# Hybrid encoder layer: output-projection weights, keys and values loaded into the low half of their split tiles, half results and x in four buffers each, and two instead of three value tiles ahead of the state-space output

## The chip, the cores and the metric

The kernel runs on one core of one Trainium2 chip. The metric is the device time of one execution in microseconds (us); lower is better. Times given here are the median of three runs, and one further execution was recorded by the hardware profiler. The engines are PE (TensorE: matrix products, with its weight loads shown apart as PEld), DVE (VectorE), ACT (ScalarE), POOL (GpSimd) and SP (SyncE, which only issues transfers). Each engine works through its own instructions in order. Sixteen DMA engines move the data.

## The reference

One layer on x of shape (1, 1024, 1024) in float32, three residual sub-layers. Only the first two matter here.

```python
h = rms_norm(x, mix_pre_g); proj = h @ w_in            # u 512 | q 512 | k 512 | v 512 | 8 gates
y_ssm = s5_mixer(u, ...)                               # diagonal state space, gelu, gated (glu)
y_fox = forgetting_attention(q, k, v, f_logit)         # 8 heads of 64, causal
y_mix = concatenate([rms_norm(y_ssm, ssm_out_g), rms_norm(y_fox, fox_out_g)])
x = x + rms_norm(y_mix @ w_out, mix_post_g)            # output projection
# cross-attention: 4 heads of 256, 256 memory tokens
kv = rms_norm(mem, mem_g) @ xa_wkv                     # keys | values
x = x + rms_norm(attention(rms_norm(x, xa_pre_g) @ xa_wq, k, v) @ xa_wo, xa_post_g)
x = x + rms_norm(swiglu(rms_norm(x, ffn_pre_g)), ffn_post_g)
```

## The kernel before, in words

**Products.** A float32 operand is split into a high and a low half (`split`, L112): ACT writes `hi` as a rounded copy (L113), DVE writes `lo = src - hi` (L115, or L117 with a gain). A product is three matmuls, hi·hi, hi·lo and lo·hi (`mm3`, L122 to L124). So each weight that is loaded needs one ACT and one DVE instruction before PE can use it.

**Order.** The kernel is written as generators that are stepped against each other. A framework then schedules all instructions by its own model of the engines and by priorities, and writes a fixed order for each engine; a changed buffer count or loop can move instructions far from the edit. SP issues the loads in that fixed order, and a load whose buffer is still in use holds every load behind it on SP. POOL issues the stores. On ACT and DVE, too, an instruction that waits holds all that follow.

**Buffers.** Tiles are taken from rings: `slab` 16 buffers (8 KB in each partition), `raw` 2 (weights as they are loaded), `whl` 3 (split weights), `a` 2, `b` 2, `c` 3, `d` 1, `e` 1, `t2` 3 (half as large, shown as `t` in the trace), four PSUM banks `g`, later four more named `x`. A ring's next tile waits until the last reader of the oldest one is done.

**Stages that the change touches**, in order of time:

1. *Projection in* (`in_proj`, L869). It ends with the generator `v1`, the second half of the value columns (8 tiles of 24 matmuls with 256 columns, evicted by ACT at L316 into a `t2` tile and stored), interleaved with `ssm_out` (L635): the state-space output, in two halves of four groups of matmuls (L643, L644), each half followed by gelu (L645) and transposes. The table V1_AT says how many value tiles go ahead of each step of `ssm_out`.
2. *Forgetting attention* (`fox`, L705): scores, exponential (L739), transposes (L758, evicted at L763), products with the values (L772). Into it are paced the `fillers` (L975), at 1.02 of their steps for one of the attention: the rest of `v1`, the gate `glu`, the state-space half of the output projection (`out_ssm`, evicted at L836 and stored to `t1_d`), the memory's keys and values (`mem_tile`, 16 weights `in_wkv` through `raw` or `e`, stored to `kv_d`), and the first part of the keys' product with the query weights (`build_a`).
3. *Output projection* (L1023 to L1083). Four weights `w_out_f` are loaded into `raw` (L1026) and split into slabs `wo`. For each of eight blocks n of 128 rows: the x tile is loaded into `c` (L1060), the half result t of stage 2 from `t1_d` into `a` or `b` (L1063, two transfers of 256 KB, shown as `t_d`), two products with `wo` are added to t (DVE, L1070), squared (ACT, L1072), multiplied by a gain row (POOL, L1074; loaded from `in_post_g`), and the normalised row is added to x (DVE, L1078). `value_weights` (L1033) is interleaved: values are loaded into a `t2` tile (L1035), split into a `b` or `e` tile and multiplied with `in_wo` weights.
4. The cross-attention and the feed-forward layer follow; the change does not touch their code.

Of the kernel before, what the change touches and what calls it, by code (L numbers as in the profile page):

```python
# [9 lines left out]
F32 = mybir.dt.float32  # L10
F32R = mybir.dt.float32r
# [23 lines left out]
MAGIC = 12582912.0  # L35
RATE = 1.02
HP = 16 * (L - 1)
V1_AT = (3, 1, 1, 1, 1)
HID = ("11", "12", "22", "S1", "S2", "S3", "S4")
EVB = 13  # L40
OPB = 10
# [11 lines left out]
def layer(ctx: ExitStack, tc: tile.TileContext, a, out):  # L53
# [15 lines left out]
    def slab(shape, dt=F32R):  # L69
        return slabp.tile(shape, dt, name="slab", tag="slab")  # L70
# [4 lines left out]
    def raw(shape):  # L75
        return rawp.tile(shape, F32, name="raw", tag="raw")
# [44 lines left out]
    def mm3(ps, lh, ll, rh, rl, first, last):  # L121
        pe.matmul(ps, lh, rh, start=first, stop=False)  # L122
        pe.matmul(ps, lh, rl, start=False, stop=False)  # L123
        pe.matmul(ps, ll, rh, start=False, stop=last)  # L124
# [21 lines left out]
        return last, done  # L146

    boost = 5000
    stA, stB, stC = pool, pool, pool

    def tables(name):
# [2 lines left out]
    def load_w(src, shape, first=0, stage=None):  # L154
        w = tt(stage, [P, D]) if stage else raw([P, D])
        hl = whl([P, 2, D])
        if not first:
            sp.dma_start(out=w, in_=src)
        for cs in (slice(0, first), slice(first, D)):
            if cs.start < cs.stop:  # L160
                if first:
                    sp.dma_start(out=w[:, cs], in_=src[:, cs])
                with tc.high_priority(offset=boost):
                    split(hl[:, 0, cs], hl[:, 1, cs], w[:, cs])
        v = hl.rearrange("p t (a b) -> p t a b", b=shape)
        return v[:, 0], v[:, 1]
# [15 lines left out]
    nc_d = dram.tile([NH, S], F32, name="nc_d")  # L182
    t1_d = dram.tile([L, NC, D], F32, name="t1_d")
    kv_d = dram.tile([16, P, 256], F32, name="kv_d")
    x1_d = dram.tile([NT, P, D], F32, name="x1_d")
    x2_d = dram.tile([NT, P, D], F32, name="x2_d")
    t_d = dram.tile([8, P, 4, 512], F32, name="t_d")
# [681 lines left out]
    def in_proj():  # L869
        r_mem.append(mem_stats())  # L870
        yield from k4
        for i in range(1, 4):
            yield from qk_tile(i + 4, xH, xL, rb)
        for n, _ in enumerate(v_tiles(0, xH, xL, r_x)):
            if n % 2:
                yield
        f_gate(gate[0])
        for i in range(4):
            yield from qk_tile(i, xH, xL, rb)
        drain(gs)  # L880
        go = ssm_out()
        for n in V1_AT:
            step(v1, n)
            step(go)
        drain(go)
# [107 lines left out]
    def build_a(c):  # L993
        for t in range(2):
            Ah[c, t], Al[c, t] = slab([P, 4, 512]), slab([P, 4, 512])
        for h in range(2):
            hd = 2 * c + h
            kr = t2t([P, 2, 256])
            sp.dma_start(out=kr, in_=kv_d[2 * hd:2 * hd + 2].rearrange("d p m -> p d m"))
            kh = tt(("ea", "ba")[c][h], [P, 2, 2, 256], F32R)  # L1000
            split(kh[:, 0], kh[:, 1], kr)
            wq = [load_w(a["wqT"][2 * hd + d], P) for d in range(2)]
            ms = slice(h * 256, h * 256 + 256)
            for ft in range(0, KT, 2):
# [17 lines left out]

    wo = []  # L1023
    for i in range(4):
        w = raw([P, D])
        sp.dma_start(out=w, in_=a["w_out_f"][i])  # L1026
        hl = slab([P, 2, D])
        split(hl[:, 0], hl[:, 1], w)
        wo.append(hl)
    g_mp = gain_row(0, "d")  # L1030
    VW = {}

    def value_weights(h):  # L1033
        vr = t2t([P, 2, 256])
        sp.dma_start(out=vr, in_=kv_d[8 + 2 * h:8 + 2 * h + 2].rearrange("d p m -> p d m"))  # L1035
        vh = tt("bebe"[h], [P, 2, 2, 256], F32R)
        split(vh[:, 0], vh[:, 1], vr)
        wo_ = [load_w(a["wo"][2 * h + d], 512) for d in range(2)]
        for mt in range(2):
            VW[2 * h + mt] = slab([P, 2, D])  # L1040
        for c in range(2):
            tiles = [(mt, (x_ps if h == 3 else g_ps)([P, 512])) for mt in range(2)]
            for d in range(2):
                for mt, ps in tiles:
                    ms = slice(mt * P, mt * P + P)
                    mm3(ps, vh[:, 0, d, ms], vh[:, 1, d, ms], wo_[d][0][:, c], wo_[d][1][:, c], d == 0, d == 1)
                    yield
            for mt, ps in tiles:
                split(VW[2 * h + mt][:, 0, c * 512:c * 512 + 512], VW[2 * h + mt][:, 1, c * 512:c * 512 + 512], ps)
# [6 lines left out]
    kept = {}  # L1056
    for n, j in enumerate((3, 4, 5, 6, 7, 0, 1, 2)):
        ts = slice(j * P, (j + 1) * P)
        xt = tt("c")
        sp.dma_start(out=xt, in_=a["x"][ts, :])  # L1060
        t = tt("aab"[n % 3])
        for i in range(2):
            sp.dma_start(out=t[64 * i:64 * i + 64], in_=t1_d.rearrange("j (k s) d -> s k j d", s=16)[2 * j + i])  # L1063
        ss4, ss, r = sm(4, "ss4"), sm(1, "ss"), sm(1, "r")
        for h in range(2):
            hs = slice(h * 512, h * 512 + 512)
            ps = x_ps([P, 512])
            for k in range(4):
                mm3(ps, yf[k][:, 0, ts], yf[k][:, 1, ts], wo[k][:, 0, hs], wo[k][:, 1, hs], k == 0, k == 3)
            dve.scalar_tensor_tensor(out=t[:, hs], in0=ps, scalar=r_f[:, j:j + 1], in1=t[:, hs], op0=ALU.mult, op1=ALU.add)  # L1070
# [558 lines left out]
```

## Time and profile before

| | |
|---|---|
| median of 3 runs | 1413.33 us |
| lowest, highest run | 1409.28, 1413.37 us |
| the profiled execution: time, span | 1414.33, 1412.5 us |
| mean granted TensorE clock in it | 0.992 |
| busy in the span: PE, DVE, ACT, POOL | 1381.8, 951.9, 652.3, 379.7 us |
| DMA moved | 239.45 MB, mean 170 GB/s |

The span runs from the first to the last instruction of the profiled execution; the time also holds what lies around it. Busy time is a sum over the span, so a full PE says nothing on a single stage: there, the timeline shows each instruction with the idle time ahead of it and the instruction that ended it. The granted clock is the share of TensorE's full speed that the chip's throttle allowed. The first state-space output matmul (L643) starts at 190.3 us and the last at 224.3, the attention's scores (L730) run from 235.2 on, its last product with the values (L772) is at 489.8, and the output projection's sums (L1070, into `a`) run from 501.6 to 550.1.

### The profile page before, as it was taken

How to read it: one execution, taken by the hardware profiler on the slowest of the kernel's cores; microseconds unless marked ns; L12 is line 12 of the kernel's file. 1: busy time of each engine (PE TensorE's matmuls, PEld its weight loads, DVE VectorE, ACT ScalarE, POOL GpSimd, SP SyncE). 2: the span in 40 equal slices, each digit the busy share in tenths (PEclk: the TensorE clock that was granted, in tenths of full speed). 3: DMA queues.
4: the chain of work that ended last, by engine and by line, in shares of the span. 5: the costliest groups of instructions: out<-in, count | busy, mean ns of one | idle time of the engine just before them, and what ended most of it. 6: DMA issues, size and time to landing. Idle time of an engine off the chain costs nothing.

```text
span 1412.5 us, 20273 instructions
## 1 busy us (share of the span) xinstructions
PE 1381.8 (98%) x7353; PEld 1163.3 (82%) x7353; DVE 951.9 (67%) x1719; ACT 652.3 (46%) x1289; POOL 379.7 (27%) x430
## 2 busy tenths in 40 slices
PE   9999989999999899999999999999999999999997
PEld 7889889789889677888888788888888888888886
DVE  8949944857567668545467777877776676655566
ACT  7383345766566546433344533333333334544351
POOL 0011110011211043001021367676766661000021
PEclk9999999999999999999999999999999999999999
DMA  6235665267663665024467345554444447955544
GB/s 217 91 108 163 201 220 138 69 200 213 183 180 113 175 194 186 27 75 152 161 202 257 97 176 193 178 187 161 145 158 154 165 150 236 357 196 194 179 164 164
DMA packets 104501, 239.45 MB, mean 170 GB/s; under 512 B 11464, under 2 KB 40136, under 8 KB 104272
## 3 DMA queue, kind: packets, MB, share of 16 engines
q1 hardware_dynamic: 85872, 176.24, 40.0%
q0 software_dynamic: 18528, 61.91, 12.3%
q8 instruction: 58, 0.95, 0.3%
q14 instruction: 43, 0.35, 0.1%
HBM read 169.43 MB, written 77.33 MB: 175 GB/s over the span
## 4 chain that ended last, share of the span: by engine, by line
PE 84%; DVE 7%; issue 3%; DMA 3%; ACT 2%; POOL 0%; SPq 0%; DVEq 0%; ACTq 0%; POOLq 0%
PE x L1294 17%; PE g L1294 13%; PE x L1557 7%; PE g L1557 7%; PE g L122 7%; PE g L124 7%; PE g L123 7%; PE x L123 2%; PE x L124 2%; PE g L758 2%; PE x L122 2%; PE g L772 2%; PE s L730 1%; PE s L731 1%; DMA a<-t_d 1%
## 5 line engine op out<-in xcount | busy, mean ns | idle before, releaser
L1294 PE MATMUL x<-slab,op 128*128 128x512 f32 x984 | 233.2, 389 | 0.5 <-DVE op L115 0.5
L1294 PEld LDWEIGHTS x<-slab,op 128*128 128x128 f32 x984 | 184.7, 188 | 39.2 <-DVE op L115 1.0
L1294 PE MATMUL g<-slab,op 128*128 128x512 f32 x744 | 178.7, 389 | 0.0
L115 DVE TENSOR_TENSOR slab<-slab 128x1024 fp32r<-128x1024 f32 (+2 forms) x92 | 110.2, 1207 | 86.4 <-ACT slab L113 85.2
L1294 PEld LDWEIGHTS g<-slab,op 128*128 128x128 f32 x744 | 139.7, 188 | 29.0
L122 PE MATMUL g<-slab,whl 128*128 128x512 f32 (+1 forms) x416 | 151.4, 364 | 0.8 <-ACT slab L485 0.4
L124 PE MATMUL g<-slab,whl 128*128 128x512 f32 (+1 forms) x416 | 148.7, 358 | 0.0
L123 PE MATMUL g<-slab,whl 128*128 128x512 f32 (+1 forms) x416 | 148.3, 357 | 0.0
L113 ACT ACTIVATE slab<-slab 128x1024 fp32r<-128x1024 f32 (+2 forms) x92 | 94.7, 1036 | 108.6 <-DMA slab<-hs_d 80.8
L1557 PE MATMUL g<-slab 128*128 128x512 f32 x462 | 126.6, 389 | 0.0
L1557 PE MATMUL x<-slab 128*128 128x512 f32 x462 | 126.6, 389 | 0.0
L1557 PEld LDWEIGHTS g<-slab 128*128 128x128 f32 x462 | 86.7, 188 | 18.0
L1557 PEld LDWEIGHTS x<-slab 128*128 128x128 f32 x462 | 86.7, 188 | 18.0
L115 DVE TENSOR_TENSOR op<-slab,op 128x512 fp32r<-128x512 f32 x80 | 84.6, 1068 | 11.5 <-ACT op L113 11.3
L1370 POOL TENSOR_TENSOR wt<-wt 128x256 f32<-128x256 f32 x88 | 83.1, 944 | 21.0 <-DMA wt<-in_w_down 17.4
L122 PE MATMUL g<-whl,slab 128*128 128x256 f32 (+2 forms) x288 | 86.8, 310 | 1.7 <-ACT yt L318 0.7
L122 PEld LDWEIGHTS g<-slab,whl 128*128 128x128 f32 x416 | 78.6, 189 | 12.0 <-ACT whl L113 0.6
L124 PEld LDWEIGHTS g<-slab,whl 128*128 128x128 f32 x416 | 78.4, 189 | 11.6 <-DVE whl L115 0.2
L123 PEld LDWEIGHTS g<-slab,whl 128*128 128x128 f32 x416 | 78.6, 189 | 10.6
L113 ACT ACTIVATE op<-slab 128x512 fp32r<-128x512 f32 x80 | 50.0, 628 | 79.9 <-PE g L1294 38.0
L124 PE MATMUL g<-whl,slab 128*128 128x256 f32 (+2 forms) x288 | 86.0, 299 | 0.0
L123 PE MATMUL g<-whl,slab 128*128 128x256 f32 (+2 forms) x288 | 85.7, 298 | 0.0
(397 smaller groups left out, 2890.3 us busy)
## 6 DMA issues: line engine op xcount, KB each, us to landing
hs_d<-ev POOLq DMA_DIRECT2D x77, 256.0 KB, 2.6
slab<-hs_d SPq DMA_DIRECT2D x35, 512.0 KB
wt<-in_w_down SPq DMA_DIRECT2D x44, 256.0 KB
wt_d<-wt POOLq DMA_DIRECT2D x22, 512.0 KB, 5.1
slab<-in_w_gate SPq DMA_DIRECT2D x20, 512.0 KB
slab<-in_w_up SPq DMA_DIRECT2D x20, 512.0 KB
slab<-wt_d SPq DMA_DIRECT2D x20, 512.0 KB
wd_d<-in_w_down SPq DMA_DIRECT2D x33, 256.0 KB
```

The lines of the kernel that those rows point to most:

```text
L113: first = act.activation(out=hi, in_=src, func=AF.Copy, scale=1.0 if mul is None else mul)
L115: (lo_eng or dve).tensor_tensor(out=lo, in0=src, in1=hi.bitcast(F32), op=ALU.subtract)
L122: pe.matmul(ps, lh, rh, start=first, stop=False)
L123: pe.matmul(ps, lh, rl, start=False, stop=False)
L124: pe.matmul(ps, ll, rh, start=False, stop=last)
L730: pe.matmul(ps[:, c0:c1], qt, ka[:, 0, c0:c1], start=True, stop=False)
L731: pe.matmul(ps[:, c0:c1], qt, ka[:, 1, c0:c1], start=False, stop=not dg)
L758: pe.transpose(tp[:, k], sc[:, (k0 + k) * P:(k0 + k + 1) * P], ident)
L772: pe.matmul(yp[hh * 64:hh * 64 + 64, c0:], w, pts[2 * hp + hh, qc][:, k, c0:], start=k == 0, stop=k == nk - 1, tile_position=(0, 64 * hh))
L1294: pe.matmul(ps, x[:, k], y[:, k], start=first and k + n == 0, stop=k == 3 and n == 2, skip_group_check=not first)
L1370: pool.tensor_tensor(out=o, in0=x, in1=y, op=ALU.subtract)
L1557: pe.matmul(banks[n][j], xo[:, u, js], wo[:, v], start=ends[0] and k == 0, stop=ends[1] and k == 2, skip_group_check=onto is not None)
```

## The change

Four edits.

- V1_AT is (2, 1, 1, 1, 1) in place of (3, 1, 1, 1, 1): two value tiles go ahead of the first state-space output; the last value tile is done as a filler of the attention.
- A DRAM tensor `wof_d` gets a copy of the four `w_out_f` weights, DRAM to DRAM, issued on SP after the last load of a `w_f` weight in the front. In stage 3 the weights are loaded from it into the low half of their slab and split in place, without `raw`.
- Keys are loaded into the low half of their split tile (an `e`, `a` or `b` tile), values into a `t2` tile that becomes their low half, with a second `t2` tile for the high half. Before, both went through a `t2` tile of their own, and the values' halves lay in a `b` or `e` tile.
- In the output projection the half results alternate over the rings `a` and `b` (2 + 2 buffers; before `a`, `a`, `b`), and x uses `e` for every fourth block and `c` for the others (1 + 3; before `c` alone). These loads are ordered behind the last load of the output weights.

```diff
-V1_AT = (3, 1, 1, 1, 1)
+V1_AT = (2, 1, 1, 1, 1)
...
+    fetched = []
...
         if not first:
-            sp.dma_start(out=w, in_=src)
+            fetched.append(sp.dma_start(out=w, in_=src))
...
+    wof_d = dram.tile([4, P, D], F32, name="wof_d")
...
         for i in range(1, 4):
             yield from qk_tile(i + 4, xH, xL, rb)
+            if i == 3:
+                with tc.issue_after(fetched[-1].ins):
+                    for j in range(4):
+                        sp.dma_start(out=wof_d[j], in_=a["w_out_f"][j])
...
-            kr = t2t([P, 2, 256])
+            kh = tt(("ea", "ba")[c][h], [P, 2, 2, 256], F32R)
+            kr = kh[:, 1].bitcast(F32)
             sp.dma_start(out=kr, in_=kv_d[2 * hd:2 * hd + 2].rearrange("d p m -> p d m"))
-            kh = tt(("ea", "ba")[c][h], [P, 2, 2, 256], F32R)
             split(kh[:, 0], kh[:, 1], kr)
...
     for i in range(4):
-        w = raw([P, D])
-        sp.dma_start(out=w, in_=a["w_out_f"][i])
         hl = slab([P, 2, D])
+        w = hl[:, 1].bitcast(F32)
+        wo_read = sp.dma_start(out=w, in_=wof_d[i])
         split(hl[:, 0], hl[:, 1], w)
...
-        vr = t2t([P, 2, 256])
+        vh, vl = t2t([P, 2, 256], F32R), t2t([P, 2, 256], F32R)
+        vr = vl.bitcast(F32)
         sp.dma_start(out=vr, in_=kv_d[8 + 2 * h:8 + 2 * h + 2].rearrange("d p m -> p d m"))
-        vh = tt("bebe"[h], [P, 2, 2, 256], F32R)
-        split(vh[:, 0], vh[:, 1], vr)
+        split(vh, vl, vr)
...
-        xt = tt("c")
-        sp.dma_start(out=xt, in_=a["x"][ts, :])
-        t = tt("aab"[n % 3])
-        for i in range(2):
-            sp.dma_start(out=t[64 * i:64 * i + 64], in_=t1_d...[2 * j + i])
+        t = tt("ab"[n % 2])
+        with tc.issue_after(wo_read.ins) if n else ExitStack():
+            for i in range(2):
+                sp.dma_start(out=t[64 * i:64 * i + 64], in_=t1_d...[2 * j + i])
+        xt = tt("ec"[n % 4 > 0])
+        with tc.issue_after(wo_read.ins):
+            sp.dma_start(out=xt, in_=a["x"][ts, :])
```

In the changed kernel line numbers are higher: L316 is L318, L645 is L647, L739 is L741, L763 is L765, L836 is L838, L1026 is L1033, L1060 is L1071, L1063 is L1068, L1070 is L1078, L1078 is L1086.

How the order moves at the places that the prediction speaks of follows; a row is an instruction's place in its engine's order, its line, operation, tiles and shape.

ACT at the end of stage 1, before: three value tiles (L316; `t` is the `t2` ring) are evicted ahead of the first gelu (L645).

```order
106 L113 ACTIVATE t_1939<-a 128x512
107 L316 ACTIVATE t_1985<-g,r_x 128x256
108 L626 ACTIVATE slab<-b 64x8x112 x2
109 L316 ACTIVATE t_2013<-g,r_x 128x256
110 L316 ACTIVATE t_2041<-g,r_x 128x256
111 L645 ACT_TABLE_LOAD
112 L645 ACTIVATE slab<-g 128x4x8x16 x4
113 L316 ACTIVATE t_2110<-g,r_x 128x256
```

The same place after:

```order
106 L113 ACTIVATE t_1944<-a 128x512
107 L318 ACTIVATE t_1990<-g,r_x 128x256
108 L628 ACTIVATE slab<-b 64x8x112 x2
109 L318 ACTIVATE t_2018<-g,r_x 128x256
110 L647 ACT_TABLE_LOAD
111 L647 ACTIVATE slab<-g 128x4x8x16 x4
112 L318 ACTIVATE t_2087<-g,r_x 128x256
```

One eviction fewer stands ahead of the gelu. On PE the order before is 49 value matmuls, eight pairs of L643 and L644, 10 value matmuls, four pairs, 13 value matmuls, four pairs; after, it is 25, twelve pairs, 23, four pairs.

ACT in stage 2, at the first split of a `wkv` weight (`whl<-raw`), before:

```order
185 L782 ACTIVATE d<-g 128x256
186 L836 ACTIVATE t_2720<-g,r_s 128x256 x2
187 L836 ACTIVATE t_2837<-g,r_s 128x256
188 L763 ACTIVATE slab<-g 128x4x128
189 L113 ACTIVATE whl<-raw 128x1024
190 L739 ACTIVATE c,nlr<-c,nlr 128x896
```

After:

```order
183 L784 ACTIVATE d<-g 128x256
184 L137 ACTIVATE rsy<-sv_s,epsc 128x8
185 L138 ACTIVATE rsy<-rsy 128x8
186 L765 ACTIVATE slab<-g 128x4x128
187 L113 ACTIVATE whl<-raw 128x1024
188 L741 ACTIVATE c,nlr<-c,nlr 128x896
189 L838 ACTIVATE t_2739<-g,r_s 128x256 x2
```

The L836 (now L838) evictions moved from ahead of the split to behind it.

SP between stages 2 and 3, before:

```order
101 L1063 DMA a<-t_d 64x1x1024 x2
102 L1026 DMA raw<-in_w_out_f 128x1024
103 L1035 DMA t_6060<-kv_d 128x2x256
104 L1063 DMA b<-t_d 64x1x1024 x2
105 L1060 DMA c<-in_x 128x1024 x2
106 L1063 DMA a<-t_d 64x1x1024 x2
107 L1026 DMA raw<-in_w_out_f 128x1024 x2
108 L158 DMA raw<-in_wo 128x1024
109 L1060 DMA c<-in_x 128x1024
110 L158 DMA raw<-in_wo 128x1024 x4
111 L947 DMA d<-in_post_g 128x1024
```

After:

```order
99 L1068 DMA a<-t_d 64x1x1024 x2
100 L159 DMA raw<-in_wo 128x1024 x2
101 L1033 DMA slab<-wof_d 128x1024 x4
102 L1071 DMA e<-in_x 128x1024
103 L1068 DMA b<-t_d 64x1x1024 x2
104 L1071 DMA c<-in_x 128x1024 x2
105 L1068 DMA b<-t_d 64x1x1024 x2
106 L1071 DMA c<-in_x 128x1024
107 L1068 DMA a<-t_d 64x1x1024 x2
108 L159 DMA raw<-in_wo 128x1024 x2
109 L953 DMA d<-in_post_g 128x1024
```

The four output weights stand together ahead of all x loads and of all but the first half result; four blocks of x and half results are now ahead of the later `in_wo` weights and of the gain row.

More of the change, by code (lines that the diff above doesn't have):

```diff
@@ L1045, in value_weights @@
                     ms = slice(mt * P, mt * P + P)
-                    mm3(ps, vh[:, 0, d, ms], vh[:, 1, d, ms], wo_[d][0][:, c], wo_[d][1][:, c], d == 0, d == 1)
+                    mm3(ps, vh[:, d, ms], vl[:, d, ms], wo_[d][0][:, c], wo_[d][1][:, c], d == 0, d == 1)
                     yield
@@ L1058, in layer @@
         ts = slice(j * P, (j + 1) * P)
-        xt = tt("c")
-        sp.dma_start(out=xt, in_=a["x"][ts, :])
-        t = tt("aab"[n % 3])
-        for i in range(2):
-            sp.dma_start(out=t[64 * i:64 * i + 64], in_=t1_d.rearrange("j (k s) d -> s k j d", s=16)[2 * j + i])
+        t = tt("ab"[n % 2])
+        with tc.issue_after(wo_read.ins) if n else ExitStack():
+            for i in range(2):
+                sp.dma_start(out=t[64 * i:64 * i + 64], in_=t1_d.rearrange("j (k s) d -> s k j d", s=16)[2 * j + i])
+        xt = tt("ec"[n % 4 > 0])
+        with tc.issue_after(wo_read.ins):
+            sp.dma_start(out=xt, in_=a["x"][ts, :])
         ss4, ss, r = sm(4, "ss4"), sm(1, "ss"), sm(1, "r")
```

## Prediction

> **What bounds the kernel now.** I read the engine table first.
>
> ```profile
> span 1412.5 us, 20273 instructions
> PE 1381.8 (98%) x7353; PEld 1163.3 (82%) x7353; DVE 951.9 (67%) x1719; ACT 652.3 (46%) x1289; POOL 379.7 (27%) x430
> ```
>
> TensorE is busy 98% of the span. The change adds or removes no arithmetic, so it can only touch what PE loses: idle time (at most 1412.5 − 1381.8 = 30.7 us) and time at a reduced clock. So I next listed the waits by engine, with PE first, and then the tensor engine's timeline for the row behind each of those gaps. The bracket is the idle time ahead of the row and who ended it.
>
> ```profile
> 184.47 0.28 PE L122 MATMUL g<-whl,slab 128*128 128x256 f32 x1
> 184.59 0.28 PE L123 MATMUL g<-whl,slab 128*128 128x256 f32 x1
> ...
> 190.35 0.39 PE L643 MATMUL g<-slab 128*128 128x128 f32 x2
> ...
> 190.79 0.39 PE L643 MATMUL g<-slab 128*128 128x128 f32 x2
> ...
> 198.60 0.80 PE L643 MATMUL g<-slab 128*128 128x128 f32 x2 [3.33 <-ACT t L316]
> 205.36 0.49 PE L643 MATMUL g<-slab 128*128 128x128 f32 x2 [0.56 <-ACT t L316]
> 207.88 0.39 PE L122 MATMUL g<-whl,slab 128*128 128x256 f32 x1 [0.46 <-ACT slab L645]
> ...
> 282.47 0.66 PE L758 MATMUL g<-ident,c 128*128 128x128 f32 x4 [1.51 <-ACT d L782]
> 289.51 1.11 PE L772 MATMUL g<-slab 128*64 128x256 f32 x4 [2.37 <-ACT t L836]
> ...
> 487.22 1.29 PE L772 MATMUL g<-slab 128*64 128x256 f32 x6 [1.54 <-ACT slab L763]
> 523.34 0.50 PE L122 MATMUL x<-slab 128*128 128x512 f32 x1 [1.87 <-DVE a L1070]
> 549.13 0.80 PE L122 MATMUL g<-whl,b 128*128 128x512 f32 x1 [2.00 <-DVE slab L115]
> ```
>
> A 256-column matmul starts every 0.12 us (184.47, 184.59), and a pair of L643 and L644 rows takes 0.44 us (190.35 to 190.79), so a v tile of 24 matmuls is 2.88 us and an output group of four pairs 1.78 us. Short gaps also cost clock. The table of stretches shows it (us; busy time and count of each engine; granted clock; DMA share, GB/s):
>
> ```profile
> 195.00:200.00 5.00, 1.67 (x9) 1.47 (x8) 0.00 (x0) 0.47 (x1) 0.54 (x1) 0.74 1.03 419
> 475.00:480.00 5.00, 5.00 (x38) 3.79 (x35) 3.97 (x7) 1.93 (x5) 0.00 (x0) 1.00 0.94 286
> 485.00:490.00 5.00, 3.46 (x21) 2.18 (x20) 2.89 (x2) 2.17 (x4) 1.49 (x1) 0.75 0.46 142
> 490.00:495.00 5.00, 5.00 (x23) 4.16 (x23) 2.17 (x3) 2.75 (x4) 0.24 (x1) 0.90 0.76 241
> 550.00:555.00 5.00, 4.21 (x14) 2.51 (x13) 5.00 (x9) 3.97 (x13) 1.28 (x1) 0.76 0.36 116
> ```
>
> **The change part by part. Two v tiles ahead.** The stall at 198.60 waits for L316, the eviction of a v tile. The chain of waits says what that eviction waited for:
>
> ```profile
> 189.63 8.34 DMA qk_d<-t
> ...
> 198.07 0.48 ACT t L316
> ...
> 202.38 0.21 PE g L124
> ...
> 207.23 0.61 ACT slab L645
> ```
>
> The eviction wants a `t` tile whose write to DRAM lands at 197.97. The third v tile and the last output groups stand behind it. After the change the order on PE is: one v tile and one matmul, three groups, the other 23 matmuls, the fourth group, and so on; the fourth group takes the bank that the second v tile leaves. I replay this. The first tile and one matmul end at 184.47 + 25 × 0.12 = 187.5. The first group needs its T matrix, which in the old run was there by 190.35 at the latest; I take the middle, 189.0. Three groups end at 194.3, the 23 matmuls at 197.1. The fourth group cannot start before the same write lands and the eviction is done: 198.07 + 0.48 = 198.55. It ends at 201.1 (between 200.3 at full clock and 202.3 at the pace of the old one, which took from 198.60 to 202.38). The gelu of its result then frees a bank 0.65 us later, as from 207.23 to 207.88. So v tile three starts at 201.8, where the old kernel starts tile four at 207.88. The deferred tile still has to be done: 2.88 us later. Gain 207.88 − 201.8 − 2.88 = **3.2 us**, with ends 2.0 and 4.0. Nothing is gained if a later buffer of the same ring is written late too.
>
> **Where the tile goes.** The fillers start with it, so everything after it moves by one tile against the attention. On ACT the first split of a `wkv` weight now stands ahead of an exponential and of L836 evictions that used to be before it. In the old run that split waits for its transfer:
>
> ```profile
> 281.32 4.87 DMA raw<-in_wkv
> 286.22 1.06 ACT whl L113
> ```
>
> ACT does nothing while it waits, and PE then waits for L836 (2.37 us at 289.51). With fewer evictions done before it, the same wait holds more of the four `g` banks. The two gaps here sum to 3.9 us; the reshuffle could heal 1.5 of it (the first gap) or add 3 (the excess of the 4.87 us transfer over the 1.51 us gap, rounded down). I take a loss of **1.0 us**.
>
> **Output weights by copy, into the slab.** In the old run the third and fourth loads wait for one of two `raw` buffers and stand on the SP queue behind loads of x and half results:
>
> ```profile
> 470.06 3.38 SPq L1060 DMA_DIRECT2D c<-in_x  x2
> 474.52 1.22 SPq L1063 DMA_DIRECT2D a<-t_d  x2
> 475.84 1.23 SPq L1026 DMA_DIRECT2D raw<-in_w_out_f  x2
> 484.41 1.06 ACT L113 ACTIVATE slab<-raw 128x1024 fp32r<-128x1024 f32 x1 [6.41 <-DMA raw<-in_w_out_f]
> 486.58 0.59 ACT L763 ACTIVATE slab<-g 128x512 f32<-128x512 f32 x1
> ```
>
> ACT stands 6.41 us at that split with L763 behind it, and PE's gap at 487.22 is L763's. Now the four loads need only their slab, stand together ahead of x, and L763 stands ahead of the last two splits on ACT. The gap goes: 5.00 − 3.46 = 1.54 us, and the clock behind it, 0.25 × 3.46 + 0.10 × 5.00 = 1.37 us. Together **2.9 us**; low end 1.5 if another wait throttles the clock there anyway. The order of the splits on DVE is the same four, so no work is added.
>
> The copy itself (four transfers of 512 KB, read and written) is issued once the last `w_f` weight of the front is fetched, and the queues there are empty:
>
> ```profile
> 55.00:60.00 5.00, 5.00 (x23) 4.13 (x22) 5.00 (x6) 0.75 (x2) 0.00 (x0) 1.00 0.03 7
> 60.00:65.00 5.00, 5.00 (x31) 4.42 (x30) 4.97 (x3) 1.74 (x5) 0.00 (x0) 1.00 0.00 0
> 67.19 8.88 SPq L328 DMA_DIRECT2D raw<-in_w_v  x2
> ```
>
> I cost it at nothing. Its cover is this empty stretch; 4.2 MB at the 419 GB/s of the busiest row above is 10 us, and that is what it could delay the next weights by if the stretch were not empty.
>
> **Half results and x in four buffers each.** The half result `t` had three buffers, and its last transfers came late, one of them here:
>
> ```profile
> 532.69 7.37 DMA a<-t_d
> DVE a L1070 <- DMA a<-t_d: 6.6, 2, 5.7
> 525.00:545.00 20.00, 20.00 (x89) 16.53 (x89) 15.84 (x27) 10.25 (x37) 10.54 (x10) 1.00 0.75 231
> 545.00:555.00 10.00, 7.14 (x23) 4.33 (x21) 9.75 (x17) 7.76 (x25) 4.49 (x3) 0.83 0.52 178
> ```
>
> The second row (waits between 500 and 560 us: total, times, longest) says that VectorE lost 6.6 us to these loads. It feeds both PE gaps: the one at 523.34 directly (L1070), and those from 549 on through its backlog, for it is idle for 4 us before 545 and full (9.75 of 10 us) after it. With two buffers more, loads four to eight are issued one block earlier. The prize is 1.87 us, 10.00 − 7.14 = 2.86 us of idle from 545 to 555 and 0.17 × 7.14 = 1.2 us of clock there, together 5.9 us. Against it: VectorE remains the fullest engine behind PE here and works in order, and the new order puts four loads of x and six of half results ahead of the later `wo` weights and of the gain row. If the weights come late instead, the loss is bounded by the nearest row, a gap like that of 549 (2 us). Between 5.9 gained and 2 lost I take two thirds of the prize, **4.0 us**, since the row of 6.6 us exceeds what is to be healed.
>
> **Keys and values in place.** No instruction is added: the load goes to the half that the split later overwrites. Values now hold two of three `t2` tiles until their matmuls end, so the next value load waits for the one before it; keys hold their `a`, `b` or `e` buffer from the load on. The cover is work PE has in hand, as the 20.00 us of 20.00 from 525 to 545 show. From 0 to 2 lost (a gap like 549's); I take **0.5 us**.
>
> **Sum.** −3.2 + 1.0 − 2.9 − 4.0 + 0.5 = −8.6 us on the profiled execution's 1414.33 us (1.8 us of it outside the span): 1405.7. That execution lies 1.0 us above the median of 1413.33, and one of the three runs at 1409.28, so I say **1406 us**. A change below 0.3% (4.2 us) cannot be told from none.
>
> **The clock, by the skill.** After a gap of 1.54 us the granted clock fell to 0.75, after 2.00 us to 0.76. The Trainium skill, "TensorE: Matmul & The Clock Gate", section "HAM oscillation — how this bites in real kernels", gives as its rule that only idle gaps longer than about 3.4 us throttle. None of the gaps above is that long, so this case's trace does not agree.
>
> **Rivals.**
> - *Gaps cost idle time alone* (the clock dips whatever the order). Then the front gives its change of idle: 3.33 + 0.56 + 0.46 before, 1.5 + 1.45 after, so −1.4; the rest is +1.0 − 1.5 − 3.2 (two thirds of 4.73) + 0.5. Sum −4.6: **1410**. For it: the low clock at 195 began inside a gap. Against it: each row with a reduced clock above holds or follows a gap. The rule named above would lead here. Chance 0.05.
> - *All of it lands*: −4.0 − 1.5 − 2.9 − 5.9 + 0 = −14.3, so **1400 to 1402**. For it: the gaps have one cause each. Against it: ACT's wait for `wkv` is still there and has more behind it. 0.15.
> - *VectorE, not the loads, holds the output projection.* It is 9.75 of 10 us busy at 545. Then only 1 us of the 5.9 is gained, and the front gives its low end: −2.0 + 1.0 − 2.9 − 1 + 0.5 = −4.4 and, with ACT's wait on `wkv` at its +3, −2.4: **1410 to 1412**. 0.27.
> - *Slower: the bunched loads starve the value weights.* Four loads of x (512 KB) and six of half results (256 KB) are 3.7 MB; at the 286 GB/s of the row at 475 they take 13 us, and the fourth `wo` weight and the gain row stand behind them. It decides once these come later than PE uses them now; the present loads are issued here:
>
> ```profile
> 488.42 11.44 SPq L158 DMA_DIRECT2D raw<-in_wo  x4
> 499.95 0.38 SPq L947 DMA_DIRECT2D d<-in_post_g  x1
> ```
>
>   Issued from 476 on, as the last pair of output weights was, the bunch ends at 489, and a weight of 4.87 us (the `wkv` row, the same size) is there by 494, ahead of the 499 at which the present four are issued. At the 142 GB/s of the row at 485 the bunch ends at 502 and the weight lands at 507: PE stands for 8 us, with 2.5 us of clock behind it (0.25 of ten). Then −3.2 + 1.0 − 2.9 + 10.5 = +5.4 us, **1420**. Against it: three of the weights are now fetched before the bunch. The Trainium skill, "DMA: Bandwidth & Descriptors", section "Issuing engines are not separate DMA queues", speaks for it: all transfers share the same 16 engines and interleave, so loads that start earlier take their bandwidth from others; the row at 475, 0.94 of the share, agrees that there is no slack there. 0.10.
>
> **Numbers.** The forecast, sum −8.6, has 0.43; its own range is 1403 to 1409. With the whole gain (0.15) and a fifth of the VectorE case, faster by over 0.3% (below 1409.1) is 0.63; within 0.3% 0.27; slower 0.10. The range from 1400 to 1414 leaves out the slower rival and about as much again at its two ends.
>
> **What would show it.** Right: in the changed profile the wait of ACT for the `raw` load is gone at 484 and no PE row of L772 waits for L763 there; the wait of VectorE for half results is below 2 us; the front's fourth group starts at 198 to 199 with a gap under 2 us ahead of it, and the fox attention's first rows come 3 us earlier relative to the work done. Wrong: a gap behind L836 or the first `wkv` split above 4 us, a PE row between 490 and 515 that waits for `whl` or a value load, or a VectorE that is still full behind 545.

## The result, and the profile after

| | before | after |
|---|---|---|
| median of the runs on one chip | 1410.48 us (8 runs) | 1417.12 us (8 runs) |
| lowest, highest | 1405.75, 1413.39 | 1415.19, 1422.13 |
| the profiled execution: time, span | 1414.33, 1412.5 | 1418.36, 1416.6 |

The ratio is 1.0051, 95% interval 1.0031 to 1.0072: the change is **slower by some 7 us**. The forecast was 1406 us, the range 1400 to 1414. The prediction expected four gaps on PE to shrink. Those at 198, 487 and 523 did; in place of the fourth, at 549, stood one of 11.07 us.

The engine table of the page of the changed kernel:

```profile
span 1416.6 us, 20283 instructions
PE 1378.9 (97%) x7353; PEld 1161.8 (82%) x7353; DVE 951.5 (67%) x1719; ACT 652.0 (46%) x1289; POOL 381.9 (27%) x430
```

PE has the same 7353 matmuls and is busy 37.7 us short of its span, where it was 30.7. The tensor engine's timeline of the changed kernel, the rows with a gap that answer to those shown of before:

```profile
190.43 0.46 PE L645 MATMUL g<-slab 128*128 128x128 f32 x2 [1.47 <-DMA slab<-T_d]
199.34 0.49 PE L645 MATMUL g<-slab 128*128 128x128 f32 x2 [0.56 <-ACT t L318]
201.86 0.38 PE L122 MATMUL g<-whl,slab 128*128 128x256 f32 x1 [0.46 <-ACT slab L647]
...
274.92 0.50 PE L732 MATMUL s<-slab,a 128*128 128x512 f32 x1 [1.99 <-DVE nlr L739]
...
285.94 0.40 PE L760 MATMUL g<-ident,c 128*128 128x128 f32 x1 [2.48 <-ACT t L838]
...
518.59 0.73 PE L124 MATMUL g<-whl,t 128*128 128x512 f32 x2 [0.79 <-DVE t L115]
550.58 0.79 PE L122 MATMUL g<-whl,t 128*128 128x512 f32 x1 [11.07 <-ACT t L113]
...
761.25 0.50 PE L122 MATMUL g<-slab,whl 128*128 128x512 f32 x1 [0.39 <-ACT whl L113]
```

The last row is the same instruction in both kernels; before it stood here:

```profile
756.93 0.50 PE L122 MATMUL g<-slab,whl 128*128 128x512 f32 x1 [0.39 <-ACT whl L113]
```

From 757 (761) on the two executions run alike: 1412.5 − 756.93 = 655.6 us to the end before, 1416.6 − 761.25 = 655.4 after. Of the 4.3 us between the rows, 1.3 have nothing to do with the change: they are there at 127 us (a short gap of PE ahead of the same matmul stands at 127.10 and 128.44), and 1.2 of them already where SP issues the `w_f` loads (42.00 and 43.24), ahead of the copy at 50.17. The other 3.0 us are the change in these two executions.

The new gap of 11.07 us is the largest of the whole program. PE waits there for the split of a value tile (`t<-t`, L113). The value had long been loaded; ACT came late to it. SP's, ACT's and DVE's timelines of the changed kernel:

```profile
528.14 0.38 SPq L1006 DMA_DIRECT2D a<-kv_d  x1
...
540.56 0.63 ACT L113 ACTIVATE a<-a 128x512 fp32r<-128x512 f32 x1 [10.19 <-DMA a<-kv_d]
549.91 0.61 ACT L113 ACTIVATE t<-t 128x512 fp32r<-128x512 f32 x1
...
541.23 0.69 DVE L115 TENSOR_TENSOR a<-a 128x512 fp32r<-128x512 f32 x1 [10.47 <-ACT a L113]
```

ACT stood for 10.19 us and DVE for 10.47 us at the split of the fourth key, `a<-a`, which waited for its load. The view of line L1006 gives the time from issue to landing (least, median, most) for two of the four key loads in this kernel, those into `a`:

```profile
DMA to landing us min/median/max: 2.6/7.5/12.3
```

The load of 528.14 is the one of 12.3 us: it lands at 540.4. The one of 2.6 us is the second key's, issued at 441.20. The load of 528.14 could not be issued earlier, for an `a` tile that holds a half result came free only then (its last reader, L1086, starts at 526.83 and takes 1.28 us). The stretches around it (us; busy time and count of PE, PEld, DVE, ACT, POOL; granted clock; DMA share, GB/s):

```profile
485.00:490.00 5.00, 5.00 (x34) 4.21 (x31) 1.58 (x4) 1.22 (x3) 0.74 (x1) 1.00 0.99 283
...
520.00:525.00 5.00, 5.00 (x24) 4.14 (x23) 3.68 (x10) 2.47 (x11) 3.69 (x4) 1.00 1.00 357
525.00:530.00 5.00, 5.00 (x24) 4.14 (x23) 4.47 (x8) 2.76 (x11) 3.06 (x3) 1.00 0.90 238
...
535.00:540.00 5.00, 4.51 (x20) 3.39 (x19) 0.00 (x0) 0.00 (x0) 0.00 (x0) 1.00 0.63 206
540.00:545.00 5.00, 0.00 (x0) 0.00 (x0) 3.65 (x7) 2.87 (x8) 1.35 (x1) 0.71 0.02 7
545.00:550.00 5.00, 0.00 (x0) 0.00 (x0) 3.81 (x9) 3.31 (x13) 1.99 (x2) 0.50 0.62 197
550.00:555.00 5.00, 4.42 (x10) 3.42 (x11) 4.88 (x7) 2.86 (x8) 4.26 (x2) 0.50 0.04 12
555.00:560.00 5.00, 5.00 (x27) 4.34 (x26) 3.39 (x6) 3.98 (x8) 0.20 (x1) 0.93 0.68 210
```

From 535 to 540 nothing runs but PE, on work it had in hand; then PE runs out. The DMA engines are full or nearly so when the key's load is issued (shares of 1.00 and 0.90); later in its flight they are not (0.74 and 0.63 in the two stretches from 530 to 540). The gap costs 11.1 us and the clock after it 0.50 × 4.42 + 0.07 × 5.00 = 2.6 us.

Why the split stood there is a matter of order. ACT's order of the changed kernel at the place (no time is in it):

```
425 L113 ACTIVATE slab<-g 128x512
426 L1080 ACTIVATE yt,ss_5712<-b 128x256 x2
427 L113 ACTIVATE a<-a 128x512
428 L137 ACTIVATE rsy<-ss,epsc 128x1
...
433 L113 ACTIVATE b<-b 128x512
...
437 L1080 ACTIVATE yt,ss_5842<-b 128x256 x2
438 L113 ACTIVATE t_5906<-t_5907 128x512
```

The split of the fourth key (427) is ahead of the squares of the last two blocks (L1080) and of the value's split (438), though nothing needs that key before the output projection is over. In the kernel before, keys came through a spare `t2` tile. The fourth key's load and its split there:

```profile
526.72 0.38 SPq L999 DMA_DIRECT2D t<-kv_d  x1
...
548.50 0.63 ACT L113 ACTIVATE a<-t 128x512 fp32r<-128x512 f32 x1 [0.95 <-DVE c L1078]
```

The load was issued only 1.4 us earlier than in the changed kernel; but its split stood 22 us behind it and waited for no load. So it is the place of the split, more than the time of the load, that changed. The first key is held in the changed kernel too: its split at 379.76 kept ACT waiting for 4.52 us, and PE was busy throughout (5.00 of 5.00 us in each stretch from 365 to 380).

### The profile page after: what moved, and what is told of

It is laid out like the page before. It is cut to its first block, busy times and chain, and to the rows that moved or that the text cites. A ratio compares the mean times of both kernels' runs of the same rounds, so it can differ in the third digit from the quotient of the medians.

```text
span 1416.6 us, 20283 instructions
## 1 busy us (share of the span) xinstructions
PE 1378.9 (97%) x7353; PEld 1161.8 (82%) x7353; DVE 951.5 (67%) x1719; ACT 652.0 (46%) x1289; POOL 381.9 (27%) x430
## 3 DMA queue, kind: packets, MB, share of 16 engines
q0 software_dynamic: 18528, 61.91, 12.3%
## 4 chain that ended last, share of the span: by engine, by line
PE 59%; DVE 0%; ACT 0%; issue 0%; DVEq 0%; ACTq 0%
PE x L1302 17%; PE g L1302 13%; PE x L1565 7%; PE g L1565 7%; PE g L124 2%; PE g L122 2%; PE g L123 2%; PE x L123 2%; PE x L124 2%; PE x L122 2%; PE g L1098 1%; PE g L1209 1%; DVE whl L115 0%; ACT whl L113 0%; DVE x L1545 0%
## 5 line engine op out<-in xcount | busy, mean ns | idle before, releaser
L115 DVE TENSOR_TENSOR slab<-slab 128x1024 fp32r<-128x1024 f32 (+2 forms) x96 | 115.3, 1208 | 85.9 <-ACT slab L113 83.9
L113 ACT ACTIVATE slab<-slab 128x1024 fp32r<-128x1024 f32 (+2 forms) x96 | 99.1, 1037 | 108.4 <-DMA slab<-hs_d 79.2
L113 ACT ACTIVATE op<-slab 128x512 fp32r<-128x512 f32 x80 | 50.0, 628 | 80.1 <-PE x L1302 38.2
```

What stands on the lines that cost most here:

```text
L113: first = act.activation(out=hi, in_=src, func=AF.Copy, scale=1.0 if mul is None else mul)
L115: (lo_eng or dve).tensor_tensor(out=lo, in0=src, in1=hi.bitcast(F32), op=ALU.subtract)
```

## The experiments

Two theories were set against each other first. **BLOCK**: the fourth key's split stands in ACT's and DVE's order ahead of work that is due, and holds it until the key's late load lands. **BUNCH** (the prediction's slower rival in a wider form): the loads brought forward fill the DMA engines, so whatever is needed next comes late.

### Key splits late

Loads, buffers and their order as in the changed kernel; the splits of keys three and four stand behind the output projection's last row on ACT and DVE.

```diff
+            with ExitStack() as late:
+                for ins in x1_row:              # last Exp and last x row of the loop over n
+                    late.enter_context(tc.issue_after(ins.ins))
                 split(kh[:, 0], kh[:, 1], kr)
```

> The changed kernel with one thing moved: the splits of the third and fourth keys stand on ACT and DVE behind the last row of the output projection; all loads, their order and buffers are as in the changed kernel. Theory BLOCK (the fourth key's load is issued only when its `a` buffer comes free at 528 us, lands 12 us later, and ACT and DVE, which work in order, stand at its split with the squares, the value split and the row sums behind it): the gap of 11.1 us at 550.6 falls below 3 us and its loss of clock (0.5 x 4.4 + 0.07 x 5 = 2.5 us) with it; 1417 - 10 to 13 = 1404 to 1407 us. Theory BUNCH (the earlier loads of x and half results fill the DMA engines, so what is needed next is late whatever stands in front of it): the loads are untouched, so a gap of 5 us or more stays between 530 and 560; 1411 to 1418 us.

Measured: **0.9972** of the kernel before (0.9958 to 0.9986), 1407.66 us beside 1411.53. Against the changed kernel that is 0.9972 / 1.0051 = 0.992, or 11 us. SP's row for the key, its time to landing, and PE's row at the old gap:

```profile
527.19 0.38 SPq L1006 DMA_DIRECT2D a<-kv_d  x1
...
DMA to landing us min/median/max: 2.7/7.6/12.5
...
540.29 0.50 PE L122 MATMUL g<-whl,t 128*128 128x512 f32 x1 [1.74 <-ACT t L113]
```

The load is as late as before the move (12.5 us) and the gap is 1.74 us instead of 11.07. The order of all instructions on SP, POOL and PE is the same in both kernels; on ACT the two splits are all that moved, on DVE three neighbours shifted by a few places with them. So BLOCK is shown, and BUNCH as the cause of this gap falls: the late load does no harm by itself. The time came out 0.7 us above the range that BLOCK gave.

### Keys back, keys and values back, four buffers back

```diff
-            kh = tt(("ea", "ba")[c][h], ...); kr = kh[:, 1].bitcast(F32)
+            kr = t2t([P, 2, 256]); ...; kh = tt(("ea", "ba")[c][h], ...)
```

> The changed kernel with the keys loaded into a `t2` tile again, as before the change; values, output weights, four buffers and two v tiles stay. BLOCK: the key load no longer waits for an `a` buffer, but `t2` has three buffers and each pair of value halves takes two, so keys and values now wait for each other; gap gone if the loads come early enough: 1404 to 1408 us. BUNCH: stall of 5 us or more stays: 1411 to 1418 us.

Measured: 0.9990 (0.9972 to 1.0008), 1410.0 us; 0.6% below the changed kernel. The time lies between the two ranges; no gap of 5 us is left, which speaks against BUNCH. The gaps left on PE in the output projection are short:

```profile
518.67 0.73 PE L124 MATMUL g<-whl,t 128*128 128x512 f32 x2 [1.42 <-DVE t L115]
541.47 0.50 PE L122 MATMUL g<-whl,t 128*128 128x512 f32 x1 [1.88 <-ACT t L113]
```

With the values' code undone as well (`vr` in a `t2` tile, halves in `b` or `e`):

> The changed kernel with keys and values as before the change (a `t2` tile each, split into `b` or `e`); output weights, four buffers and two v tiles stay. If the in-place keys are the whole of the loss: 1403 to 1407 us, faster than the kernel before by 0.3 to 0.5%. If the values in place were worth something of their own: slower than the run with only the keys back. BUNCH: 1411 to 1418 us.

Measured: 1.0020 (1.0004 to 1.0037), 1414.84 us: slower than with only the keys back, so the values' new place is worth something beside the four buffers, whose half results and x now go through `b` and `e` as well. The time is in BUNCH's range, but no gap of 5 us is there. The profiled execution was the slowest of its kernel, 1420.08 us:

```profile
524.24 0.79 PE L122 MATMUL x<-slab 128*128 128x512 f32 x1 [3.66 <-DVE b L1078]
...
553.00 0.50 PE L122 MATMUL g<-whl,b 128*128 128x512 f32 x1 [2.57 <-DVE slab L115]
```

And the loop over n with its old tiles (`c` for x, `a`, `a`, `b` for t), all else changed:

> The changed kernel with three buffers each for half results and x again (order of loads as before the change); keys and values in place stay. BUNCH: the stall near 550 goes, 1406 to 1410 us. BLOCK: the fourth key still has to wait for an `a` buffer behind the half results, and its load lands late: a gap of 4 us or more stays and the old gaps at 523 and 549 come back, 1412 to 1420 us.

Measured: 1.0007 (0.9991 to 1.0022), 1413.1 us. Both theories missed here: the time lies in BLOCK's range, but by luck, for none of the gaps that it named is there. The gap near 550 is 2.1 us (at 542.98), near what BUNCH had, but not because less was loaded: SP's order of this kernel has the fourth key's load behind all half results, and its split behind them on ACT. The time is not what BUNCH had, since another gap came up:

```profile
476.96 1.22 PE L122 MATMUL x<-slab 128*128 128x512 f32 x4 [2.50 <-ACT slab L113]
...
542.98 0.79 PE L122 MATMUL g<-whl,t 128*128 128x512 f32 x1 [2.11 <-ACT t L113]
```

So the block at 550 is made by two edits together: keys in place, and the order that came with the four buffers.

### Each part alone on the kernel before

The table alone:

```diff
-V1_AT = (3, 1, 1, 1, 1)
+V1_AT = (2, 1, 1, 1, 1)
```

> The kernel before with V1_AT = (2, 1, 1, 1, 1) alone. Theory FRONT (the traces of the changed kernel and of its variants): the deferred value tile saves 4.4 us by 208 us and the attention's first weeks of work, 265 to 295 us, give back 1.6 to 2.4 us by waits and a lower clock; net 2 to 3 us: 1408 to 1410 us beside 1411.5, 0.998 to 0.9985. Rival: the tile's time is only moved and the waits behind it take all of it: 1411 to 1412 us, ratio 1.

Measured: 1.0008 (0.9991 to 1.0024). The gain is not there. Its timeline and one stretch:

```profile
189.53 0.46 PE L643 MATMUL g<-slab 128*128 128x128 f32 x2 [1.91 <-DVE b L624]
202.58 0.39 PE L122 MATMUL g<-whl,slab 128*128 128x256 f32 x1 [0.46 <-ACT slab L645]
190.00:195.00 5.00, 5.00 (x32) 5.00 (x32) 1.79 (x3) 2.03 (x3) 1.68 (x4) 0.66 0.96 276
```

After a gap of 1.91 us the clock was 0.66; in the changed kernel 1.47 us came ahead of the same group, and the third value tile began 0.7 us earlier (201.86), although that execution ran 1.3 us late up to there.

The output weights alone (copy, load into the slab, split in place):

> The kernel before with the output weights by copy into the slab alone. Theory: ACT's wait of 6.4 us at 484 goes and with it PE's gap of 1.5 us and the clock behind it, 2.9 us: 1408 to 1409.5 us, and the copy at 50 to 60 us costs nothing. Rival: with x and half results in three buffers and not held behind the output weights, these loads still come late, in another place: 1411 to 1413 us.

Measured: 0.9990 (0.9971 to 1.0010), 1411.05 us: nothing that can be told from zero, and in the rival's range. It also showed something in the front, where its order is that of the kernel before:

```profile
196.15 0.49 PE L645 MATMUL g<-slab 128*128 128x128 f32 x2 [0.34 <-ACT t L318]
195.63 0.47 ACT L318 ACTIVATE t<-g,r_x 128x256 f32<-128x256 f32 x1 [2.93 <-DMA qk_d<-t]
```

The gap of 3.33 us, on which the first term of the prediction rests, is 0.34 us here. The write that ends it was issued at 190.17 and the eviction that waits for it started 5.5 us later; in the profile of before it was 8.4 us (189.63, 198.07).

Four buffers alone (the loop over n alone, with the rings `a`, `b` and `e`, `c`):

> The kernel before with half results alternating over `a` and `b` and x over `e` and `c` alone. Theory COLLIDE (the run with keys and values back was 1414.8 us although it has the gains of the front and of the output weights, 5 us): the split values are in `b` and `e`, which are now rings of half results and x as well, so loads wait for values and the reverse; slower than before, 1414 to 1420 us, with gaps of 3 us or more between 515 and 560. Theory of the prediction (two more buffers bring the loads forward): 1406 to 1408 us.

Measured: 1.0024 (1.0009 to 1.0040), slower. PE's largest gap in the loop is the value tile's, in `e`:

```profile
539.91 0.69 PE L122 MATMUL g<-whl,e 128*128 128x512 f32 x1 [4.28 <-ACT e L113]
```

Keys and values in place alone:

> The kernel before with keys and values loaded into the low half of their split tiles alone. If the in-place key blocks only where its load stands among the half results of the new order: the fourth key's load stands behind all of them here, no gap over 4 us between 520 and 560, 1408 to 1412 us. If it blocks by itself: a gap of 5 us or more there, 1414 to 1420 us.

Measured: **1.0053** (1.0033 to 1.0073), 1418.24 us: as slow as the whole change. The time is in the second range, but the gap at 523 stays under the 5 us named there, and no expectation named the gap in the attention. PE's gaps, and ACT's row in the attention:

```profile
370.92 0.39 PE L122 MATMUL g<-whl,slab 128*128 128x256 f32 x1 [3.07 <-ACT t L836]
...
523.86 0.79 PE L122 MATMUL x<-slab 128*128 128x512 f32 x1 [4.33 <-DVE a L1070]
...
369.39 0.63 ACT L113 ACTIVATE e<-e 128x512 fp32r<-128x512 f32 x1 [6.43 <-DMA e<-kv_d]
```

The first key, loaded in place into `e`, holds ACT for 6.4 us in the middle of the attention, with an eviction (L836) behind it that PE wants: the same block at another key. From 360 to 380 us idle time and reduced clock (reckoned as after the gap above, by stretches of five us) cost 4.5 us here and nothing in the kernel before. The gap at 523 is at the place of the old one of late half results, and longer: in the second profile of the kernel before, shown below, PE came to this place at 519.3, here at 519.5, and waited 2.48 us there and 4.33 here. From 500 to 570 idle time and clock cost 12.6 us, against 6.2 and 6.6 in the two profiles of before. The third key's split held ACT for 3.65 us in that stretch (at 529.94) without a gap on PE. This kernel's orders differ from before's in many places from 440 on, and how the 6 us more come about is not shown.

### The front's gap again, and the table beside the late splits

> The kernel before, unchanged, for a second profile. Open since the run with the output weights alone: its order in the front is that of the kernel before, but its gap ahead of the third group of L643 was 0.3 us instead of 3.3, since the write that the eviction waits for landed 3 us earlier. If that landing is the kernel's own: 3 to 4 us again at 198. If it varies between executions: another gap, 0 to 3 us, and the gain of the two v tiles, measured against one profile, is partly luck.

The kernel before, a second profile:

```profile
198.63 0.80 PE L643 MATMUL g<-slab 128*128 128x128 f32 x2 [2.86 <-ACT t L316]
...
521.75 0.50 PE L122 MATMUL x<-slab 128*128 128x512 f32 x1 [2.48 <-DVE a L1070]
```

The execution took 1412.52 us. The gap is there again, smaller. Over the profiles with three value tiles ahead and this front order it was 3.33, 2.86, 3.78 (four buffers alone), 1.27 (keys and values alone) and 0.34 us (output weights alone). In the first four of these profiles every engine runs the same instructions in the same order up to 205 us, in the fifth the copy at 50 us is all that is added. So the gap is not a fixed part of the program; why the write lands sooner or later is not shown.

```diff
 # the changed kernel with key splits late
-V1_AT = (2, 1, 1, 1, 1)
+V1_AT = (3, 1, 1, 1, 1)
```

> The changed kernel with the key splits late and three value tiles ahead again. It tells what the table's edit is worth beside the other three. Theory FRONT, as the traces have it (4.4 us gained by 208, 2.4 us given back from 250 to 300): 2 us slower than the run with only the key splits late, 1409 to 1410 us. Theory of the run with the table's edit alone (1.0008): no difference, 1407 to 1408 us.

Measured: 0.9979 (0.9964 to 0.9994), 1406.8 us; the run with two tiles was 0.9972. No difference, so the table's edit is worth nothing that can be measured. Its trace has a front gap of 0.82 us and, in the attention, the block at the first key:

```profile
196.12 0.49 PE L645 MATMUL g<-slab 128*128 128x128 f32 x2 [0.82 <-ACT t L318]
369.37 0.58 PE L122 MATMUL g<-whl,slab 128*128 128x256 f32 x1 [3.13 <-ACT t L838]
367.83 0.63 ACT L113 ACTIVATE e<-e 128x512 fp32r<-128x512 f32 x1 [6.49 <-DMA e<-kv_d]
```

From there, the first two keys through `t2` again (`kr = t2t(...)` for c = 0):

> The changed kernel with three value tiles ahead and the late splits of the third and fourth keys, and the first two keys loaded through a `t2` tile again. The run before it (three value tiles, late splits) has a gap of 3.1 us at 369, which ends with an L838 eviction that stands on ACT behind the split of the first key; that key's load lands 6 us after its issue. Theory BLOCK, in a second place: with the load into a spare `t2` tile the gap goes; 2 to 4 us below 1406.8: 1403 to 1405 us, 0.995 to 0.997. Rival: the `t2` ring of three is shared with the evictions of the fillers and the two tiles of each value, so the wait comes back at 455 to 475: 1406 to 1409 us.

Measured: 0.9980 (0.9962 to 0.9999), 1408.16 us. The gap at 369 is gone, as BLOCK had it; the time is the same. The profiled execution had a front gap of 2.28 us instead of 0.82 and one of 2.30 at 538 instead of 0.52, so what was gained is within what executions differ by. Inconclusive on the price of the block there.

### The first `wkv` split behind the evictions

```diff
+        with tc.issue_after(evs[-1].ins) if i == 0 else ExitStack():   # evs: the L838 evictions so far
             wh, wl = load_w(a["wkv"][i], P, ...)
```

> The changed kernel with the key splits late, and the split of the first `wkv` weight ordered behind the evictions of the state-space half (L838) that the code has issued by then. Theory: ACT no longer stands for the weight's transfer with evictions behind it; the gap of 1.9 us at 285 and part of the low clock there (0.5 to 0.7 from 275 to 290, 5.5 us in all) go: 2 to 4 us below the run with only the key splits late, 1404 to 1406 us. Rival: the wait goes on to the product that needs this weight, or the clock stays low because of the 2 us gap at 274 that DVE makes: 1407 to 1409 us.

Measured: **0.9962** (0.9948 to 0.9976), 1405.62 us, the fastest of all, 5.4 us below the kernel before. Two stretches of the run with only the key splits late, then the same two of this one:

```profile
280.00:285.00 5.00, 3.34 (x17) 3.15 (x16) 1.87 (x5) 2.38 (x5) 0.00 (x0) 0.65 0.31 99
285.00:290.00 5.00, 4.74 (x25) 3.20 (x27) 4.20 (x11) 5.00 (x13) 0.80 (x2) 0.69 0.68 224
```

```profile
280.00:285.00 5.00, 5.00 (x30) 5.00 (x29) 3.61 (x8) 3.95 (x10) 0.72 (x1) 0.59 0.47 156
285.00:290.00 5.00, 5.00 (x45) 4.06 (x44) 2.90 (x11) 4.51 (x12) 0.73 (x1) 1.00 0.63 184
```

PE is busy throughout and its clock is whole again from 285 on. The gap of 1.9 us went, as expected, and part of the low clock: the same cure as for the keys, a split that waits for a load moved behind work that is ready. From 280 to 285 the clock is still 0.59, as the rival had it. In these two profiles the stretch from 250 to 300 loses 7.3 us instead of 9.9; in the ratios to the kernel before, 0.9962 beside 0.9972, the intervals overlap, so a gain in time over the key splits alone is not shown. Nor did this edit move the one split alone: two `wkv` loads stand a few places later on SP, and PE's order differs from 290 to 332.

## Why the prediction was wrong

The step that failed is **keys and values in place**, priced at 0 to 2 us lost, 0.5 taken, with "the cover is work PE has in hand". PE's work covers a late load for the matmuls that use it, but the split of the key stands on ACT and DVE, and what stands behind it there was PE's present work. The runs put the price at about 11 us (the changed kernel against the same with two splits moved), and this edit alone on the kernel before cost 0.5%, 7 to 8 us. The prediction asked for a waiting instruction what was queued behind it in two places (the `wkv` split, the `raw` load) and not in this one, though the order of the changed kernel showed the split ahead of two blocks' squares, and its own row of a half-result load of 7.37 us showed what a load takes there.

Term by term, in the two profiles, from the rows above and from what idle time and reduced clock cost in stretches of five us:

| term | predicted | measured in the profile of the changed kernel |
|---|---|---|
| two value tiles ahead | −3.2 | −4.5 by 202 us: 207.88 + 1.34 − 2.88 − 201.86 |
| the attention, 250 to 300 | +1.0 | +1.2 (8.2 to 9.4) |
| output weights | −2.9 | −2.8: idle and clock from 450 to 500 fell from 5.4 to 2.6; no gap and a clock of 1.00 at 485 |
| output projection, keys and values | −3.5 | +9.1 (idle and clock from 500 to 570: 6.2 to 15.3) |
| sum | −8.6 | +3.0, beside +3.0 between the rows at 128 and 761 |

That the sums meet to the tenth is luck: from 210 to 250 the changed kernel lost another 1.4 us, mostly in two gaps of 0.57 and 0.90 us at 231.53 and 233.71 (waits for DVE), and no row has it.

- **Front.** The replay was right in its steps: the first group did wait for T (1.47 us, 1.5 expected) and began at 190.43, 1.4 us later than forecast in an execution that ran 1.3 us late. The fourth group waited 0.56 us where 1.45 were forecast, for PE's own work and not for the write. What was wrong is that the gap to be removed was taken as a fixed part of the kernel. It differs between executions, 1.3 to 3.8 us with one and the same order up to there, and on the median of runs the edit gains nothing: 1.0008 alone, 0.9979 against 0.9972 beside the rest.
- **Attention.** The place and the sign were right. The price was too low with the key splits late (9.9 us lost from 250 to 300; 8.2 and 6.3 in the two profiles of before), and a gap that was not named came first: DVE, full, kept PE for 2.0 us at 274.
- **Output weights.** Right in these two profiles, term by term: the ACT wait of 6.41 us is gone. Alone it does not show in the time (0.9990, 0.9971 to 1.0010); its trace has other gaps from 456 to 486, where the old order of x and half results is kept, and loses 9.6 us from 450 to 500.
- **Four buffers.** VectorE's wait for half results, 6.6 us before, does not show in the changed kernel, where the loads had the time of the block to land. With the key splits late it is 2.6 us (at 538), above the 2 us that the prediction gave as its sign, and the loss from 500 to 570 is 4.3 us instead of 6.2: 1.9 us of the 4.0 taken. Without the values' new place the buffers cost time (1.0024), so as an edit of its own it was misjudged.
- **The slower rival** put its place at 499 and its mechanism in the fourth `wo` weight. That weight was in time; no gap stands between 490 and 515. Right in it was that the DMA engines have no slack there: shares of 0.99 at 485 and 1.00 at 520. The Trainium skill's "DMA: Bandwidth & Descriptors", section "Issuing engines are not separate DMA queues" (all transfers interleave on the same 16 engines), states what would make a load late there. The key's load took 12.3 us from 528 on and the second key's 2.6 us at 441, at mean shares of 0.68 (528 to 541) and 0.77 (441 to 444), so the share alone does not tell the one from the other, and the run with late splits shows that the late load does not set the time.
- **VectorE, not the loads** is not refuted. With the key splits late DVE is less busy over the whole stretch (30.5 us of 40 from 530 to 570; 34.8 before), but still full from 540 to 550 (9.7 us of 10), and of the 5.9 us in question 1.9 were gained, nearer to the 1 us of this rival than to the 4.0 taken.
- **The sum** stood on one execution of 1414.33 us; the median of all runs of before was 1410.5 to 1411.5. Some 3 us of what could be gained in that profile were not in the typical run.

Without the block, the kernel is 0.28% faster than before (0.14 to 0.42%), about 4 us, less than half of the 8.6 us forecast. That difference was measured; how it divides between the front's varying gap, the attention and the output projection is argued from single profiles.

## What to carry to other kernels

Loading into the final tile saves a buffer and ties the load to the last user of that tile. Here that moved the fourth key's load by only 1.4 us; the cost came from its split, which then stood close behind the load in the order of ACT and DVE. Before such a change, look where the first instruction on that load stands in its engine's order, and price not the load but all that waits behind it there; moving two such splits behind ready work was worth 11 us here, more than twice the 4 us that the change gains without the block. And a stall read from one profile should be seen in a second one before a term of a sum rests on it.

## What the runs showed of the hardware

- A 256 KB write (`qk_d<-t`) with the same work around it let the eviction that waits for it start 5.5, 6.5, 7.1, 8.4 and 8.8 us after its issue in five executions (the profiles of the front's gap above), at DMA shares of 0.9 to 1.0. A 256 KB load (`kv_d`) took 2.6 us at 441 and 12.3 us at 528 in one execution, at mean DMA shares of 0.77 (441 to 444) and 0.68 (528 to 541).
- Gaps below 3 us lowered the granted clock in some executions and not in others: in the kernel before it was 0.70 from 290 to 295, after a gap of 2.37 us, and 1.00 there in its second profile, after one of 2.87 us at the same place. At another place it was 0.66 in the five us after a gap of 1.91 us (the table alone) and 1.00 after one of 1.61 us (key splits late). After the gap of 11.07 us it was 0.50. The Trainium skill, "TensorE: Matmul & The Clock Gate", section "HAM oscillation — how this bites in real kernels", has the clock fall to half after idle gaps above about 3.4 us; the 0.50 agrees with the half; the 0.66 after 1.91 us and the 0.70 after 2.37 do not agree with the limit.
